# Encoder on one Trainium2 core: LayerNorm shift in one VectorE instruction, one router copy moved to ScalarE, a shorter reciprocal root

## The chip, the core and the metric

The kernel runs on one core of a Trainium2 chip. A core has five engines that work side by side, each with its own queue of instructions in a fixed order: TensorE (PE in the profile, with its weight loads as PEld), VectorE (DVE), ScalarE (ACT), GpSimd (POOL) and SyncE (SP), which here only issues DMAs. TensorE writes to PSUM, and VectorE or ScalarE carry results from PSUM to SBUF. The metric is the device time of one execution in microseconds, taken as the median of several runs.

## The reference, cut to what matters

Two layers over 512 tokens of width 1024. Each layer has a mixer (differential attention in layer 0, sparse latent attention in layer 1), a cross attention to a memory, and a mixture of 16 experts, each followed by a residual and a LayerNorm:

```
def layer_norm(x, g, b):
    mu = mean(x);  xc = x - mu
    return xc * rsqrt(mean(xc * xc) + LN_EPS) * g + b

h = layer_norm(alpha * h + mix, ln_g[i, 0], ln_b[i, 0])
h = layer_norm(alpha * h + memory_cross_attention(h, ...), ln_g[i, 1], ln_b[i, 1])
h = layer_norm(alpha * h + hierarchical_moe(h, ...), ln_g[i, 2], ln_b[i, 2])
```

The root also stands in the RMS norm that follows each head of the differential attention, and in two RMS norms of the latent attention. The mixture's router takes the normalised rows times a 1024x20 matrix, picks a group and two experts for each token, and each expert works on the tokens that chose it.

## The kernel before

Tokens are worked in 4 tiles of 128. Most matmuls are done three times with operands split in a high and a low part ("h" and "l" tiles: ScalarE writes the high part, L203 and L253, VectorE the low one, L204 and L254).

**Order of work.** The instructions of SP and GpSimd run in program order everywhere. Those of TensorE, ScalarE and VectorE are laid out by a planner ahead of the run, with its own estimate of durations, except in three places where the program's order holds: TensorE in the memory attention, all three engines in the expert loop of `moe`, and VectorE in the LayerNorm that ends `moe` (the strings `LNO` give that order: A adds the last expert, C scales, R is a root, H shifts, T turns a tile).

**The root**, `rsqrt` (L183 to L197), is computed on VectorE from an integer seed (L187 to L189) and three Newton steps. A step is L194, L195, L196 where the operand has several columns, and L192, L196 where it has one. So a root is 12 instructions with several columns and 9 with one. Each waits for the one before it. It is used by `attend` of the differential attention (4 columns, tiles rsyrms, one for each of 8 heads; L495 multiplies the head by it and L498 turns the head on TensorE), by `ln_stats` in `out_proj` (1 column, one for each of 16 tiles), by `compress` of the latent attention (2 columns, 4 times) and by the LayerNorm that ends `moe` (layer 0: 1 and 3 columns, layer 1: 2 and 2).

**`out_proj`** (L320 to L347) runs four times: after the mixer (tiles op0x in layer 0, op1x in layer 1) and after the memory attention (xp0x, xp1x). For each half hf of the columns and each tile t it projects (L248 to L250), adds the residual on VectorE (L337), and with hf = 1 takes the statistics (mean L295, squares on ScalarE L299, root), scales in place (L303) and shifts in place. The shift is `ln_shift`: VectorE does 768 of the 1024 columns (L309), GpSimd the last 256 in two instructions (L312, L313). Then:

- after the mixer, `after0` stores the tile to h_d from GpSimd's queue (L1575), and `to_T` turns it on TensorE in eight 128-column transposes (L263) for the memory attention's query projection (xq). The last two transposes read the columns of GpSimd.
- after the memory attention, `after1` stores the tile twice: to h_d from GpSimd's queue (L1584) and to acc_d from SP's (L1585). The expert loop's weight loads (cell_r, L228) stand behind the first acc_d store in SP's queue. Here `router_part` also runs: four transposes of each half (L693), a copy of the result from PSUM (first half on ScalarE L698, second half on VectorE L696), and four matmuls with the router's matrix (L701). `router_logits` (L709 to L711) puts the logits together. The scale L303 overwrites the rows that L693 reads, so it comes after the transposes.

Then VectorE works out the routing (`router`, from L740 on, and the first experts' token lists L889), and GpSimd gathers the first expert's tokens from h_d (L932), which needs all four stores to h_d. The gathered rows are turned on TensorE (L939), split, and the expert loop begins with L954.

In the LayerNorm that ends `moe` the shift already is one VectorE instruction of 1024 columns (`TLNS` = 1024).

Of the kernel before, what the change touches and what calls it, by code (L numbers as in the profile page):

```python
# [17 lines left out]
AF = mybir.ActivationFunctionType  # L18
ALU = mybir.AluOpType
# [4 lines left out]
D = 1024  # L24
# [22 lines left out]
       "A0 A1 C0 A2 R02 C1 A3 H0 H1 C2 R24 C3 H2 H3")  # L47
DSA = ("F2 E2 q0 q1 F3 E3 q2 s0 s1 q3 s2 s3 u0 u1 u2 u3 "
       "k0 k1 k2 k3 k4 k5 k6 k7 v0 v1 v2 v3 x1 a0 x2 a1 x3 a2 a3")
LNS = 768  # L50
TLNS = 1024
SCT = 4
WB = 6
RB = 3
# [11 lines left out]
def encoder(ctx: ExitStack, tc: tile.TileContext, I, out):  # L66
    nc = tc.nc
# [8 lines left out]
    def tp(name):  # L76
        return ps.tile([P, 512], F32, tag="tp", name=name, bufs=2)
# [6 lines left out]
    def t4(tag, name, shape=None, dtype=F32):  # L84
        return sb.tile(shape or [P, 1024], dtype, tag=tag, name=name, bufs=BUFS[tag])

    def t2(tag, name, shape=None, dtype=F32):
        return sb.tile(shape or [P, 512], dtype, tag=tag, name=name, bufs=BUFS[tag])
# [17 lines left out]
    def small(name, shape, dtype=F32, bufs=2):  # L106
        return sb.tile(shape, dtype, tag="_" + re.sub(r"\d+", "", name), name=name, bufs=bufs)
# [74 lines left out]

    def rsqrt(x, n, name, mul, add, room=None):  # L183

        v, y, w, yi = (small(f"rs{q}{name}", [P, room or n], I32 if q == "i" else F32)[:, 0:n] for q in "vywi")
        k = 2.0 ** 26
        nc.vector.tensor_scalar(v, x, mul * k, add * k, op0=ALU.mult, op1=ALU.add)  # L187
        nc.vector.tensor_scalar(yi, v.bitcast(I32), 1, None, op0=ALU.logical_shift_right)  # L188
        nc.vector.tensor_scalar(y.bitcast(I32), yi, -1, 0x5F3759DF - 2 ** 31, op0=ALU.mult, op1=ALU.add)  # L189
        for c in (3.0, 12.0, 768.0):  # L190
            if n == 1:
                nc.vector.scalar_tensor_tensor(w, y, v, y, op0=ALU.mult, op1=ALU.mult)  # L192
            else:
                nc.vector.tensor_tensor(w, y, y, op=ALU.mult)  # L194
                nc.vector.tensor_tensor(w, w, v, op=ALU.mult)  # L195
            nc.vector.scalar_tensor_tensor(y, w, -c, y, op0=ALU.add, op1=ALU.mult)  # L196
        return y  # L197

    def wsplit(raw, hi, lo, scale=None, chunks=1):
# [42 lines left out]
    def ts(t):  # L242
        return slice(t * P, (t + 1) * P)
# [48 lines left out]
    def ln_stats(hx, sums, name, eps=EPS):  # L292
        nmu = small(name + "m", [P, 1])
        if len(sums) == 2:
            nc.vector.tensor_scalar(nmu, sums[0], sums[1], -1.0 / D, op0=ALU.add, op1=ALU.mult)  # L295
        else:
            nc.vector.tensor_scalar(nmu, sums[0], -1.0 / D, None, op0=ALU.mult)
        ss = small(name + "s", [P, 1])
        nc.scalar.activation(junk, hx, AF.Square, bias=nmu, accum_out=ss)  # L299
        return nmu, rsqrt(ss, 1, name, 1.0 / D, eps)  # L300

    def ln_scale(hx, nmu, gb):
        nc.vector.scalar_tensor_tensor(hx, hx, nmu, gb[0], op0=ALU.add, op1=ALU.mult)  # L303

    last_shift = [None]

    def ln_shift(hx, rstd, gb, n=LNS):
        c = slice(0, n)
        last = nc.vector.scalar_tensor_tensor(hx[:, c], hx[:, c], rstd, gb[1][:, c], op0=ALU.mult, op1=ALU.add)  # L309
        if n < D:  # L310
            c = slice(n, D)
            nc.gpsimd.tensor_scalar(hx[:, c], hx[:, c], rstd, None, op0=ALU.mult)  # L312
            nc.gpsimd.tensor_tensor(hx[:, c], hx[:, c], gb[1][:, c], op=ALU.add)  # L313
        last_shift[0] = last

    def proj_part(o, oT, W, t, ks, last=False):
        mm3(o, [(oT[0](k, ts(t)), oT[1](k, ts(t)),
# [33 lines left out]
    def reload(src, name, tags="abcd", q=nc.gpsimd, t0=0):  # L351
        hx = []
        for t, tag in enumerate(tags, t0):
            x = t4(tag, f"{name}{t}")
            q.dma_start(x, src[ts(t), :])  # L355
            hx.append(x)
        return hx


    def diff_attention(x_ap):  # L360
# [92 lines left out]
        def attend(h):  # L453
# [4 lines left out]
            for t in range(NT):  # L458
# [30 lines left out]
                for kt in range(t + 1):  # L489
                    nc.tensor.matmul(po[:, 0:P], pT[:, ts(kt)], V[:, kt, :], start=kt == 0, stop=kt == t)  # L490
                nc.scalar.activation(og[:, t, :], po[:, 0:P], AF.Copy, scale=rs[:, 0:1])
                nc.scalar.activation(junk[:, 0:P], po[:, 0:P], AF.Square, scale=rs[:, 0:1],
                                     accum_out=ssq[:, t:t + 1])
            rstd = rsqrt(ssq, NT, f"rms{h}", 1.0 / P, EPS)
            nc.vector.tensor_tensor(og, og, rstd.unsqueeze(2).to_broadcast([P, NT, P]), op=ALU.mult)  # L495
            pt = tp(f"oT{h}")
# [193 lines left out]
    def router_part(R, t, hf, x, nm):  # L690
        pt = tp(f"hTf{nm}")
        for j in range(4):
            nc.tensor.transpose(pt[:, ts(j)], x[:, ts(j)], ident)  # L693
        xT = t2("e", f"hTs{nm}")
        if hf:
            nc.vector.tensor_copy(xT, pt)  # L696
        else:
            nc.scalar.activation(xT, pt, AF.Copy)  # L698
        lp = tp(f"lg{nm}")
        for j in range(4):  # L700
            nc.tensor.matmul(lp[:, 0:20], xT[:, ts(j)], R["w"][:, 4 * hf + j, 0:20], start=j == 0, stop=j == 3)  # L701
        if hf:
            R["lp"] = lp
        else:
            nc.vector.tensor_copy(R["lg"][:, t, :], lp[:, 0:20])
# [326 lines left out]
    def moe(i, R, early, before, store, after, order, first):  # L1032
        rt = router(i, R)
        xg, xT = {}, {}
# [79 lines left out]
        pg, pu, hid, pt, hs, py, R_ = {}, {}, {}, {}, {}, {}, {}  # L1114
# [4 lines left out]
        def way_in(o, cur, p, j):  # L1119
            W, n = take(p, j)  # L1120
            for v in cur:
                if j % 2 == 0:
                    o[v] = mm(f"p{'gu'[j // 2]}{name(v)}")
                ff_in(o[v], j % 2, xT[v], W)
            return n
# [17 lines left out]
        with tc.manual_schedule(engines={ENG.PE, ENG.Activation, ENG.DVE}):  # L1143
# [7 lines left out]
            for p in range(NE):  # L1151
# [11 lines left out]
                n = way_in(pg, cur, p, 0)  # L1163
                if p:
                    refill(n)
                n = way_in(pg, cur, p, 1)
# [10 lines left out]
                n = way_in(pu, cur, p, 2)  # L1177
                if p:
                    refill(n)
                n = way_in(pu, cur, p, 3)  # L1180
# [38 lines left out]
        hx = reload(acc_d, f"mhx{i}", "aaab")  # L1219
        gb = (t4("c", f"mg{i}"), t4("b", f"mb{i}"))  # L1220
# [22 lines left out]
        rstd = {}  # L1243

        def root(r):
            y = rsqrt(ss[:, r], r.stop - r.start, f"mln{i}{r.start}", 1.0 / D, EPS / ALPHA ** 2, NT)
            for t in range(r.start, r.stop):
                rstd[t] = y[:, t - r.start:t - r.start + 1]

        steps = dict(A=add, C=lambda t: ln_scale(hx[t], nmu[:, t:t + 1], gb),  # L1250
                     H=lambda t: (ln_shift(hx[t], rstd[t], gb, TLNS), store(t, hx[t])))
        before()
        with tc.manual_schedule(engines={ENG.DVE}):
            begin()
# [316 lines left out]
    for i in range(nl):  # L1571
# [29 lines left out]
        def before():  # L1601
            if i + 1 < nl:
                gT.extend([Tall("gTh"), Tall("gTl")])
                D3.extend(dsa(gT, W3))

        def store(t, h):
            if i + 1 == nl:
                nc.sync.dma_start(out[0, ts(t), :], h)
            else:
                nc.sync.dma_start(h2_d[ts(t), :], h)  # L1610

        def after2(st, hx):
# [4 lines left out]
            else:  # L1617
                D3[0](st)

        moe(i, R, early, before, store, after2, LNO[i], first)  # L1620
        if i + 1 < nl:
            D3[0](DSA)
# [28 lines left out]
```

## Time and profile before

| | |
|---|---|
| median of 3 runs | 1695.44 us (1695.03 to 1698.78) |
| the profiled execution | 1692.59 us |
| its span, first to last instruction | 1690.8 us |
| TensorE busy | 1522.3 us (90%) |
| VectorE busy | 1206.2 us (71%), 2381 instructions |
| ScalarE busy | 862.6 us (51%), 1156 instructions |
| GpSimd busy | 230.2 us (14%), 228 instructions |
| mean granted TensorE clock | 0.95 of full |

The spans of the profile count from its first instruction. The profiled execution has 1.8 us around its span, and is 0.17% below the median of the runs. In the rows further down, a time ahead of a row is its start in us from the start of the span; "idle before" is the time in which that engine had nothing to do just ahead, with what ended it.

### The profile page before, as it was taken

How to read it: one execution, taken by the hardware profiler on the slowest of the kernel's cores; microseconds unless marked ns; L12 is line 12 of the kernel's file. 1: busy time of each engine (PE TensorE's matmuls, PEld its weight loads, DVE VectorE, ACT ScalarE, POOL GpSimd, SP SyncE). 2: the span in 40 equal slices, each digit the busy share in tenths (PEclk: the TensorE clock that was granted, in tenths of full speed). 3: DMA queues.
4: the chain of work that ended last, by engine and by line, in shares of the span. 5: the costliest groups of instructions: out<-in, count | busy, mean ns of one | idle time of the engine just before them, and what ended most of it. 6: DMA issues, size and time to landing. Idle time of an engine off the chain costs nothing. (4 is left out here: it accounts for less than half of the span.)

```text
span 1690.8 us, 23295 instructions
## 1 busy us (share of the span) xinstructions
PE 1522.3 (90%) x8572; PEld 1292.7 (76%) x8572; DVE 1206.2 (71%) x2381; ACT 862.6 (51%) x1156; POOL 230.2 (14%) x228
## 2 busy tenths in 40 slices
PE   7998799698995899999996899998998699999994
PEld 7988699597784777888875757698777487888883
DVE  5555746555447998898875698836436899899795
ACT  5443646432320775775763454533322477677671
POOL 1000000011004031231210000002002222132120
PEclk9999899799996899999997999999998699999998
DMA  7210234432415798998974301024242599899883
GB/s 227 75 51 1 75 113 157 156 91 87 165 59 213 246 364 314 311 355 314 320 254 157 96 25 63 26 89 151 76 142 110 211 363 371 281 333 368 280 300 124
DMA packets 118334, 317.58 MB, mean 188 GB/s; under 512 B 23773, under 2 KB 72925, under 8 KB 93632
## 3 DMA queue, kind: packets, MB, share of 16 engines
q1 hardware_dynamic: 100400, 272.00, 45.3%
q0 software_dynamic: 17808, 43.96, 8.5%
q8 instruction: 71, 1.16, 0.3%
q14 instruction: 55, 0.45, 0.1%
HBM read 299.38 MB, written 36.70 MB: 199 GB/s over the span
## 5 line engine op out<-in xcount | busy, mean ns | idle before, releaser
L204 DVE TENSOR_TENSOR cell_l<-cell_r,cell_h 128x2048 fp32r<-128x2048 f32 x192 | 430.7, 2285 | 40.4 <-ACT cell_h L203 39.9
L203 ACT ACTIVATE cell_h<-cell_r 128x2048 fp32r<-128x2048 f32 x192 | 363.4, 1915 | 77.7 <-DMA cell_r<-in_moe_w_up_dram 17.8
L954 PE MATMUL pg<-cell_h,xh 128*128 128x512 f32 x288 | 118.9, 413 | 2.2 <-ACT xh L253 2.2
L982 PE MATMUL py<-cell_h,hsh 128*128 128x512 f32 x288 | 115.4, 401 | 1.4 <-ACT hsh L253 0.7
L954 PE MATMUL pg<-cell_l,xh 128*128 128x512 f32 x288 | 116.2, 403 | 0.0
L982 PE MATMUL py<-cell_h,hsl 128*128 128x512 f32 x288 | 112.8, 392 | 0.0
L982 PE MATMUL py<-cell_l,hsh 128*128 128x512 f32 x288 | 112.5, 390 | 0.0
L954 PE MATMUL pu<-cell_h,xh 128*128 128x512 f32 x288 | 112.0, 389 | 0.0
L954 PE MATMUL pu<-cell_l,xh 128*128 128x512 f32 x288 | 112.0, 389 | 0.0
L972 POOL DMA_INDIRECT acc_d<-y,sx x34 | 72.9, 2143 | 152.1 <-ACT y L971 103.2
L932 POOL DMA_INDIRECT xg<-h_d,sx x32 | 42.0, 1312 | 363.8 <-DVE sx L919 334.2
L253 ACT ACTIVATE xh<-xgT 128x1024 fp32r<-128x1024 f32 x36 | 36.9, 1024 | 101.6 <-PE xgT L939 95.9
L954 PE MATMUL pg<-cell_h,xl 128*128 128x512 f32 x288 | 79.8, 400 | 0.0
L954 PE MATMUL pu<-cell_h,xl 128*128 128x512 f32 x288 | 77.0, 389 | 0.0
L954 PEld LDWEIGHTS pg<-cell_h,xh 128*128 128x128 f32 x288 | 56.6, 197 | 14.1 <-ACT xh L253 3.0
L954 PEld LDWEIGHTS pg<-cell_h,xl 128*128 128x128 f32 x288 | 56.1, 195 | 12.5
L954 PEld LDWEIGHTS pg<-cell_l,xh 128*128 128x128 f32 x288 | 56.3, 195 | 11.4
L982 PEld LDWEIGHTS py<-cell_h,hsh 128*128 128x128 f32 x288 | 54.2, 188 | 13.0 <-DVE xl L254 1.0
L982 PEld LDWEIGHTS py<-cell_h,hsl 128*128 128x128 f32 x288 | 54.0, 188 | 12.5 <-DVE hsl L254 0.4
L954 PEld LDWEIGHTS pu<-cell_h,xh 128*128 128x128 f32 x288 | 54.1, 188 | 11.2
L954 PEld LDWEIGHTS pu<-cell_h,xl 128*128 128x128 f32 x288 | 54.1, 188 | 11.2
L954 PEld LDWEIGHTS pu<-cell_l,xh 128*128 128x128 f32 x288 | 54.1, 188 | 11.2
(918 smaller groups left out, 4203.9 us busy)
## 6 DMA issues: line engine op xcount, KB each, us to landing
cell_r<-in_moe_w_gate_dram SPq DMA_DIRECT2D x64, 1024.0 KB, 7.8
cell_r<-in_moe_w_up_dram SPq DMA_DIRECT2D x64, 1024.0 KB, 7.8
cell_r<-in_moe_w_down_dram SPq DMA_DIRECT2D x64, 1024.0 KB, 6.9
mhx<-acc_d POOLq DMA_DIRECT2D x8, 512.0 KB, 7.4
x<-in_x_dram SPq DMA_DIRECT2D x4, 512.0 KB, 6.7
g<-in_ln_g_dram POOLq DMA_DIRECT2D x4, 512.0 KB, 4.0
b<-in_ln_b_dram POOLq DMA_DIRECT2D x4, 512.0 KB, 3.9
op0x<-in_x_dram POOLq DMA_DIRECT2D x4, 512.0 KB, 5.2
```

The lines of the kernel that those rows point to most:

```text
L203: nc.scalar.activation(hi[:, c], raw[:, c], AF.Copy)
L204: nc.vector.tensor_tensor(lo[:, c], raw[:, c], hi[:, c].bitcast(F32), op=ALU.subtract)
L253: nc.scalar.activation(hi, src, AF.Copy)
L932: nc.gpsimd.indirect_dma_start(out=x, out_offset=None, in_=h_d[:, :], in_offset=bass.IndirectOffsetOnAxis(ap=idx[:, 0:1], axis=0), bounds_ ...
L954: nc.tensor.matmul(o, xT[l][:, a, :], W[r][:, k, :], start=a == l == r == 0, stop=a == 7 and l == 1)
L972: nc.gpsimd.indirect_dma_start(out=acc_d[:, :], out_offset=bass.IndirectOffsetOnAxis(ap=ix[:, 0:1], axis=0), in_=y, in_offset=None, bounds ...
L982: nc.tensor.matmul(o, hs[a][:, ts(2 * q + f)], Dq[b][:, f, c], start=q == f == k == 0, stop=q == f == 1 and k == 2)
```

## The change

Three edits. The shift of a LayerNorm is one VectorE instruction over all 1024 columns in every place; the two GpSimd instructions go. The router's second half is copied from PSUM by ScalarE, as the first half is. The root has one third-order step and one Newton step in place of three Newton steps: 8 instructions with one column, 10 with several.

```diff
     def rsqrt(x, n, name, mul, add, room=None):
         v, y, w, yi = (...)
-        k = 2.0 ** 26
+        k = (1024.0 / 27.0) ** 2
         nc.vector.tensor_scalar(v, x, mul * k, add * k, op0=ALU.mult, op1=ALU.add)
         nc.vector.tensor_scalar(yi, v.bitcast(I32), 1, None, op0=ALU.logical_shift_right)
         nc.vector.tensor_scalar(y.bitcast(I32), yi, -1, 0x5F3759DF - 2 ** 31, op0=ALU.mult, op1=ALU.add)
-        for c in (3.0, 12.0, 768.0):
+        for cubic in (True, False):
             if n == 1:
                 nc.vector.scalar_tensor_tensor(w, y, v, y, op0=ALU.mult, op1=ALU.mult)
             else:
                 nc.vector.tensor_tensor(w, y, y, op=ALU.mult)
                 nc.vector.tensor_tensor(w, w, v, op=ALU.mult)
-            nc.vector.scalar_tensor_tensor(y, w, -c, y, op0=ALU.add, op1=ALU.mult)
+            if cubic:
+                nc.vector.scalar_tensor_tensor(w, w, -10.0 / 3.0, w, op0=ALU.add, op1=ALU.mult)
+            nc.vector.scalar_tensor_tensor(y, w, 5.0 if cubic else -64.0 / 3.0, y, op0=ALU.add, op1=ALU.mult)
         return y
...
-    def ln_shift(hx, rstd, gb, n=LNS):
-        c = slice(0, n)
-        last = nc.vector.scalar_tensor_tensor(hx[:, c], hx[:, c], rstd, gb[1][:, c], op0=ALU.mult, op1=ALU.add)
-        if n < D:
-            c = slice(n, D)
-            nc.gpsimd.tensor_scalar(hx[:, c], hx[:, c], rstd, None, op0=ALU.mult)
-            nc.gpsimd.tensor_tensor(hx[:, c], hx[:, c], gb[1][:, c], op=ALU.add)
-        last_shift[0] = last
+    def ln_shift(hx, rstd, gb):
+        last_shift[0] = nc.vector.scalar_tensor_tensor(hx, hx, rstd, gb[1], op0=ALU.mult, op1=ALU.add)
...
         xT = t2("e", f"hTs{nm}")
-        if hf:
-            nc.vector.tensor_copy(xT, pt)
-        else:
-            nc.scalar.activation(xT, pt, AF.Copy)
+        nc.scalar.activation(xT, pt, AF.Copy)
...
-                     H=lambda t: (ln_shift(hx[t], rstd[t], gb, TLNS), store(t, hx[t])))
+                     H=lambda t: (ln_shift(hx[t], rstd[t], gb), store(t, hx[t])))
```

## Rows read from the trace of the kernel before

**Rows 1.** Busy time by stretch: us, PE, PEld, DVE, ACT, POOL, clock, DMA share, GB/s.

```profile
550.00:895.00 345.00, 333.85 (x1589) 272.87 (x1590) 303.00 (x400) 237.12 (x179) 71.78 (x54) 0.99 0.88 312
```

**Rows 2.** PE waits, 0 to 355 us: waited for, us in total, times, longest.

```profile
PE oT L498 <- DVE og L495: 17.7, 4, 4.6
```

**Rows 3.** Timeline of TensorE at the ends of the LayerNorms: start, us, engine, instruction.

```profile
371.63 0.44 PE L263 MATMUL hT<-ident,op0x 128*128 128x128 f32 x2 [1.25 <-POOL op0x L313]
...
391.36 0.88 PE L263 MATMUL hT<-ident,op0x 128*128 128x128 f32 x6 [0.98 <-DVE op0x L309]
392.95 0.44 PE L263 MATMUL hT<-ident,op0x 128*128 128x128 f32 x2 [0.72 <-POOL op0x L313]
...
908.56 1.97 PE L263 MATMUL gT<-ident,mhx 128*128 128x128 f32 x8 [12.69 <-DVE mhx L309]
...
1173.33 0.44 PE L263 MATMUL hT<-ident,op1x 128*128 128x128 f32 x2 [0.42 <-POOL op1x L313]
```

**Rows 4.** Timeline of VectorE, after the memory attention of layer 0.

```profile
514.59 0.69 DVE L696 COPY hTsxp<-hTfxp 128x512 f32<-128x512 f32 x1 [0.30 <-PE hTfxp L693]
515.20 1.28 DVE L303 SCALAR_TENSOR_TENSOR xp0x<-xp0x,xp0ln0m,g 128x1024 f32<-128x1024 f32 x1
...
531.59 0.16 DVE L740 TENSOR_REDUCE rt<-lgs 128x4 f32<-128x16 f32 x1
...
539.37 0.16 DVE L889 TENSOR_SCALAR ix<-pi 128x1 int32<-128x1 f32 x1 [0.28 <-PE pi L887]
```

**Rows 5.** Timeline of GpSimd, same stage.

```profile
533.56 0.61 POOL L1584 DMA_DIRECT2D h_d<-xp0x  x1 [0.30 <-POOL xp0x L313]
...
542.48 1.08 POOL L932 DMA_INDIRECT xg<-h_d,ix  x1 [6.46 <-DVE rt L792]
```

**Rows 6.** Line 932, 500 to 560 us: the gather's wait in its queue, ns.

```profile
L932 POOLq EVENT_SEMAPHORE  x3: 17/43/7857, 533.7 to 542.3; - x3
```

**Rows 7.** The chain that ended last, near its end: start, us, what.

```profile
1682.64 0.17 DVE rswmln L194
```

**Rows 8.** Timeline of VectorE, one root with 4 columns (attention) and one with 1.

```profile
329.34 0.16 DVE L196 SCALAR_TENSOR_TENSOR rsyrms<-rswrms,rsyrms 128x4 f32<-128x4 f32 x1
329.53 0.69 DVE L495 TENSOR_TENSOR og<-og,rsyrms 128x512 f32<-128x512 f32 x1
...
389.83 0.22 DVE L192 SCALAR_TENSOR_TENSOR rswop0ln<-rsyop0ln,rsvop0ln 128x1 f32<-128x1 f32 x1
390.09 0.16 DVE L196 SCALAR_TENSOR_TENSOR rsyop0ln<-rswop0ln,rsyop0ln 128x1 f32<-128x1 f32 x1
```

**Rows 9.** Line 309 of VectorE: ns min/median/max, first and last start, shapes.

```profile
L309 DVE SCALAR_TENSOR_TENSOR mhx<-mhx,rsymln,mb x8: 1274/1280/1285, 907.2 to 1685.5; 128x1024 f32<-128x1024 f32 x8
L309 DVE SCALAR_TENSOR_TENSOR op0x<-op0x,rsyop0ln,b x4: 1008/1019/1066, 368.2 to 390.3; 128x768 f32<-128x768 f32 x4
```

**Rows 10.** Timeline, a GpSimd addition and the VectorE instruction beside it, layer 0's mixer.

```profile
386.62 0.87 POOL L313 TENSOR_TENSOR op0x<-op0x,b 128x256 f32<-128x256 f32 x1
...
386.82 1.75 DVE L303 SCALAR_TENSOR_TENSOR op0x<-op0x,op0ln3m,g 128x1024 f32<-128x1024 f32 x1
```

**Rows 11.** Busy time by stretch (columns as in Rows 1), xq matmuls of layers 0 and 1.

```profile
396.00:399.00 3.00, 3.00 (x18) 3.00 (x17) 0.10 (x1) 0.00 (x0) 0.00 (x0) 0.59 0.00 0
...
1176.00:1180.00 4.00, 4.00 (x36) 4.00 (x35) 0.48 (x1) 0.60 (x1) 0.00 (x0) 1.00 0.01 2
```

**Rows 12.** Line 698 of ScalarE: ns min/median/max, first and last start, shapes.

```profile
L698 ACT ACTIVATE hTsxp<-hTfxp x8: 597/598/598, 489.4 to 1287.2; 128x512 f32<-128x512 f32 x8
```

**Rows 13.** SyncE's queue, the store that stands ahead of the weight loads.

```profile
519.15 0.33 SPq L1585 DMA_DIRECT2D acc_d<-xp0x  x1
```

**Rows 14.** Busy time by stretch (columns as in Rows 1), where the transfers end.

```profile
541.00:542.00 1.00, 0.00 (x0) 0.00 (x0) 0.90 (x6) 0.00 (x0) 0.00 (x0) 0.50 0.34 135
```

**Rows 15.** DMA queues, 517 to 545 us: packets, MB, share of 16 engines.

```profile
q1 hardware_dynamic: 1152, 6.29, 58.1%
q0 software_dynamic: 666, 2.17, 20.3%
```

More of the change, by code (lines that the diff above doesn't have):

```diff
@@ L49 @@
        "k0 k1 k2 k3 k4 k5 k6 k7 v0 v1 v2 v3 x1 a0 x2 a1 x3 a2 a3")
-LNS = 768
-TLNS = 1024
 SCT = 4
```

## The prediction

> **What bounds the kernel now.** I read the busy time by stretch first, then the waits of TensorE, then the timelines of the places that those waits name, and the chain that ended last for the end. In the expert loops, about 345 us in layer 0 and nearly as long in layer 1, TensorE is busy 334 of 345 us [rows 1]: no edit touches them, and what begins earlier ahead of them ends earlier by as much. The changed instructions matter only in the joints between, and there are three kinds.
>
> In the attention of layer 0 TensorE stands still 17.7 us in four waits for the head that VectorE multiplies by its root [rows 2]. Four heads of eight wait; the other four are covered by other matmuls.
>
> At the ends of the LayerNorms TensorE waits for rows to turn [rows 3]. After layer 0's mixer the first tile's last two transposes wait 1.25 us for GpSimd, and the last tile waits 0.98 us for VectorE's shift and then 0.72 us for GpSimd's. In layer 1 one wait of 0.42 us for GpSimd is left. At the start of layer 1 the wait of 12.69 us ends with a shift, ahead of which stands a root.
>
> After the memory attention VectorE works nearly without a pause from 514.59 to 531.59 us, where the routing begins, and the first token list is ready some 8 us later [rows 4]. GpSimd issues its last store to h_d at 533.56 and gathers at 542.48 [rows 5]; the gather had waited 7.86 us in the queue, until 542.3 [rows 6]. The list was there by 539.6, so it is the store's landing that ends this wait last. Layer 1 repeats the pattern. At the very end the root's instructions stand one by one on the chain [rows 7]; the order string puts two roots there.
>
> **The root.** With several columns an instruction takes a step of 0.19 us (from 329.34 to 329.53) [rows 8], and two fall away: 0.38 us. With one column, the dropped step is one L192 (0.26 us from 389.83 to 390.09) and one L196, and the third-order step adds one of L196's kind: 0.26 us saved. Where it lies on the path: four heads, 4 x 0.38 = 1.5 us; two roots of the end, 0.8 us; the one-column root ahead of the 12.69 us wait, 0.3 us. The four roots of the latent attention's norms are worth 0 to 1.5 us; no wait that I show ends with them, so I take 0.4 us. The other roots lie beside other work and count nothing; the worst they could cost is nothing, since each is shorter.
>
> **The shift after the mixers.** VectorE's instruction grows from 1.019 to 1.280 us [rows 9]: +0.26 us for each tile, which the shorter root gives back. GpSimd's two instructions vanish, and with them the wait of the last two transposes. Besides, an L303 that ran beside a GpSimd addition took 1.75 us in place of 1.28 [rows 4, 10], so 0.47 us of stall goes too. Layer 0, first tile: 1.25 us, and +0.26 - 0.26 = 0. Last tile: 0.72 us, and of the 0.98 us before it 0.26 + 0.47 - 0.26 = 0.47; together 1.2 us. After that tile the granted clock was 0.59 on the mean, so mostly at the lower level of 1.2 GHz (18 matmuls in 3 us); in layer 1, where the pauses ahead of it were shorter by about those amounts, it stayed at 1.00, 2.4 GHz (36 in 4 us) [rows 11]. 18 x (0.167 - 0.111) = 1.0 us; I take it, since the pauses that are left come near to layer 1's. Layer 0: 3.45 us, between 1.25 (the last tile waits on something else) and 4. Layer 1: 0.42 us, taken as 0.4. The h_d store behind it now waits for VectorE alone; it is read long after and hidden.
>
> **The stage after the memory attention**, twice. From VectorE's 17.0 us [rows 4] go four copies at a step of 0.61 us (514.59 to 515.20), 2.4 us; stalls beside four GpSimd additions, from 0 to 4 x 0.47, taken as three, 1.4 us; two roots, half hidden in each other, 0.3 us. Four longer shifts add 1.0 us. Net 3.1 us: the routing begins near 528.5 and the first list is ready near 536.4. The copy itself takes 0.60 us on ScalarE [rows 12] against 0.69 on VectorE, so the matmuls behind it lose nothing; behind it in ScalarE's queue stands at most the next tile's squares, which the root of that tile waits for. Should a copy stand behind such a square it is late once, by about its 0.6 us or two of them, which the next tile's transposes would feel: 0 to 1.2 us, taken as 0, because the scale L303 waits for the transposes and not for the copy.
>
> The last store to h_d goes out right after the last shift, near 528.8 in place of 533.56: 4.8 us earlier. If it lands as long after its issue as before (542.3 - 533.56 = 8.7 us), the gather starts 4.8 us earlier: the upper end. But the transfers are what is full here. They start with the first store to acc_d, at 519.15 [rows 13], behind which the weight loads stand in SP's queue, and end a third of the way into 541 to 542 [rows 14]. That first store follows the first tile's shift, and in the new order it goes out near 517.2: L303 begins 0.6 us earlier without the copy, and the store no longer waits for GpSimd's second instruction. If the same bytes need the same 22.2 us, they end 2.0 us earlier: the lower end. The lists, 3 us earlier, are ready before that. I take 2.9 us, nearer to the lower end because the bytes have to pass in any case: 5.8 us for both layers.
>
> How the two queues share is open. In this stage GpSimd's queue q0 moved 666 packets of 2.17 MB and SP's q1 1152 of 6.29 MB [rows 15], and the last store took 8.7 us though at most one other stood ahead of it in q0. The Trainium skill, "DMA: Bandwidth & Descriptors", section "Queues, rings and completion order", says that a DMA engine goes round the queues that have work, one packet of one queue at a time. By that rule the h_d stores would overtake the weight loads and the sum would be the first rival's, 1676.5 us; by the 8.7 us of the row, which bear it out in part only, it is the one here.
>
> **The sum.** 1.5 + 0.8 + 0.3 + 0.4 + 3.45 + 0.4 + 5.8 = 12.65 us. The profiled execution's 1692.6 us become 1679.9; it lies 0.17% below the median of the runs, so on the median 1695.4 - 12.7 = 1682.7, given as 1683. Changes of under 0.2% (3.4 us) are about what a measurement of this kernel can't tell from none.
>
> **Rivals.** *The stores overtake the loads.* The packets are 3.3 KB on q0 and 5.5 KB on q1 [rows 15]. If the queues take turns packet by packet, q0 has 3.3 of 8.8, 37% of 381 GB/s (8.46 MB in 22.2 us), and its last two stores of 0.52 MB each are through in 7.4 us, near 534 if the first of them goes out near 526. Then the list, near 536.4, starts the gather, 6.1 us earlier than 542.48, and two stages give 12.2 in place of 5.8: 1676.5 us. For it: more of q0's stores are queued early. Against it: the 8.7 us of the last store. Chance 0.13.
>
> *The transfers end where they did.* If something other than the first shift holds back the loads, or the loads, now ahead, delay the stores, the two stages give nothing: 1683 + 5.8 = 1688.5 us. For it: transfers were still running in 541 to 542 [rows 14] with the gather behind them. Chance 0.15.
>
> *The planner lays the engines out anew.* Outside the hand-ordered parts it works from its own durations, and shorter roots and other engines give it other input. Place: the heads of layer 0's attention. Price: a head whose turn is put right behind its root costs 17.7 / 4 = 4.4 us [rows 2]; four heads have none of this now. With two or three of them uncovered, 8.8 to 13.3 us are lost, and the time is 1691.5 to 1696: no change within 0.2% (chance 0.12, with smaller disorders elsewhere). With all four, 17.7 us, it is 1700 us and slower; that is the point from which it decides (chance 0.08). For it: the planner did uncover four heads already. Against it: the edit removes two of the twelve small instructions and moves nothing that a head waits for.
>
> The forecast itself has 0.52, with a range of its own from 1677 to 1689: the lower and upper ends above (layer 0's joint 1.25 to 4, each routing stage 2.0 to 4.8, the latent norms 0 to 1.5). Faster: 0.52 + 0.13 + 0.15 = 0.80; same 0.12; slower 0.08. The range, 1674 to 1693, takes in both faster rivals and the lower edge of no change, and leaves out some 0.18.
>
> **What would show it.** Right: 2326 instructions on VectorE (2381 - 17 - 30 - 8), 1164 on ScalarE and 196 on GpSimd; no wait of TensorE for GpSimd in front of L263; the four waits behind L495 each 0.4 us shorter; no L303 over 1.3 us; the clock at 1.00 after layer 0's last tile; routing begun 3 us sooner after the first tile's transposes and the gather 2 to 5 us sooner; two roots 0.8 us shorter at the end; the expert loops as long as before. Wrong: more or longer waits behind L495, a gather that still waits as long after the first shift, a router matmul that waits on ScalarE, or an expert loop of another length.

## The result and the profile after

| | kernel before | changed kernel |
|---|---|---|
| median of the runs | 1696.80 us (5 runs, 1695.03 to 1698.78) | 1686.36 us (5 runs, 1682.32 to 1688.29) |
| ratio | 1 | 0.9933, 95% interval 0.9919 to 0.9947 |
| profiled execution | 1692.59 us, span 1690.8 | 1682.87 us, span 1680.7 |
| instructions on VectorE / ScalarE / GpSimd | 2381 / 1156 / 228 | 2325 / 1165 / 196 |

By the ratio the kernel is 11.4 us faster (0.67%, 9.0 to 13.7); the two medians differ by 10.4. The forecast was 12.65 us, 1683 us on the median before. The profile after, read at the places that the forecast named. First TensorE's waits behind the root of the attention, one row for each head that waits (in brackets the wait and what ended it):

```profile
130.70 0.71 PE L493 MATMUL oT<-ident,og 128*128 128x128 f32 x4 [4.20 <-DVE og L490]
...
182.46 1.08 PE L493 MATMUL oT<-ident,og 128*128 128x128 f32 x4 [4.18 <-DVE og L490]
...
308.99 1.09 PE L493 MATMUL oT<-ident,og 128*128 128x128 f32 x4 [10.30 <-DVE og L490]
...
326.50 1.09 PE L493 MATMUL oT<-ident,og 128*128 128x128 f32 x4 [3.61 <-DVE og L490]
```

Three of the four that [rows 2] sums are 0.39 to 0.40 us shorter (in the kernel before they were 4.60, 4.57 and 4.00). The third grew from 4.49 to 10.30; a wait of 2.95 us for an exponential, which stood just ahead of it in the kernel before, is in that:

```profile
304.98 2.07 PE L466 MATMUL sc<-kS,qab 128*128 128x512 f32 x4 [2.95 <-ACT p L475]
...
311.54 1.12 PE L498 MATMUL oT<-ident,og 128*128 128x128 f32 x4 [4.49 <-DVE og L495]
```

So the four together grew, from 17.7 us to 22.3.

Second, the joint after layer 0's mixer. TensorE's timeline has two long waits in it (and two of 0.69 and 0.34 us at the last tile), and none is for GpSimd:

```profile
375.33 0.38 PE L249 MATMUL xq<-hTh,xwq00h 128*128 128x256 f32 x1 [2.17 <-ACT hTh L254]
...
378.94 0.58 PE L250 MATMUL xq<-hTl,xwq00h 128*128 128x256 f32 x1 [3.22 <-DVE hTl L255]
```

The waits of [rows 3] behind the shift are gone, but the first query product now waits for the high and the low part of tile 1. ScalarE's and VectorE's timelines say why:

```profile
371.11 1.90 ACT L204 ACTIVATE xwq01h<-xwq01r 128x2048 fp32r<-128x2048 f32 x1
372.91 1.89 ACT L204 ACTIVATE xwq02h<-xwq02r 128x2048 fp32r<-128x2048 f32 x1
374.71 0.58 ACT L254 ACTIVATE hTh<-hT 128x512 fp32r<-128x512 f32 x1
...
375.92 2.29 DVE L205 TENSOR_TENSOR xwq02l<-xwq02r,xwq02h 128x2048 fp32r<-128x2048 f32 x1
...
378.20 0.69 DVE L255 TENSOR_TENSOR hTl<-hT,hTh 128x512 fp32r<-128x512 f32 x1
```

Both engines split the weights of two later query products first. In the kernel before, one part of tile 1 stood between the two splits, and TensorE's two waits for tile 1, both for low parts, were 1.6 and 2.0 us:

```profile
376.42 1.90 ACT L203 ACTIVATE xwq01h<-xwq01r 128x2048 fp32r<-128x2048 f32 x1
378.22 0.57 ACT L253 ACTIVATE hTh<-hT 128x512 fp32r<-128x512 f32 x1
379.56 1.91 ACT L203 ACTIVATE xwq02h<-xwq02r 128x2048 fp32r<-128x2048 f32 x1 [0.77 <-PE op0o L249]
...
381.40 0.39 PE L249 MATMUL xq<-hTl,xwq00h 128*128 128x256 f32 x1 [1.63 <-DVE hTl L254]
...
385.05 0.39 PE L249 MATMUL xq<-hTl,xwq00h 128*128 128x256 f32 x1 [1.96 <-DVE hTl L254]
```

The clock behind the last tile, 0.59 in [rows 11], is at full speed here, but the stretch at the lower level is not gone: it now stands behind the wait of 3.22 us (windows of layer 0; columns: stretch, busy us of PE, PEld, DVE, ACT and POOL, granted clock, DMA share, GB/s):

```profile
379.00:383.00 4.00, 4.00 (x19) 4.00 (x20) 3.86 (x10) 1.64 (x3) 0.53 (x1) 0.50 1.05 391
...
386.00:392.00 6.00, 4.97 (x40) 4.54 (x39) 2.56 (x4) 1.19 (x2) 0.53 (x1) 1.00 0.21 87
392.00:396.00 4.00, 4.00 (x35) 4.00 (x35) 0.00 (x0) 0.61 (x2) 0.00 (x0) 1.00 0.02 4
```

Over the whole joint the granted clock was 0.91 in the changed kernel and 0.96 in the kernel before:

```profile
354.90:393.23 38.33, 31.91 (x244) 31.05 (x243) 26.72 (x62) 13.02 (x19) 2.14 (x4) 0.91 0.50 167
```

```profile
359.06:399.40 40.34, 32.11 (x245) 30.42 (x244) 27.44 (x66) 13.13 (x18) 12.47 (x12) 0.96 0.48 159
```

Third, the stage after layer 0's memory attention, on SP, GpSimd and VectorE:

```profile
511.18 0.33 SPq L1577 DMA_DIRECT2D acc_d<-xp0x  x1
...
523.61 0.16 DVE L732 TENSOR_REDUCE rt<-lgs 128x4 f32<-128x16 f32 x1
...
523.99 0.53 POOL L1576 DMA_DIRECT2D h_d<-xp0x  x1 [1.45 <-DVE rt L734]
524.51 1.86 POOL L920 MEMSET xg<- 128x1024 f32 x2
...
524.72 1.68 DVE L736 TENSOR_SCALAR rt<-rt 128x16 f32<-128x16 f32 x1
...
532.27 0.16 DVE L881 TENSOR_SCALAR ix<-pi 128x1 int32<-128x1 f32 x1 [0.28 <-PE pi L879]
...
534.00 1.08 POOL L924 DMA_INDIRECT xg<-h_d,ix  x1 [7.64 <-DVE rt L771]
```

Beside [rows 4, 5, 13] the first store to acc_d goes out 7.97 us sooner, the last one to h_d 9.57, the list is ready 7.10 and the gather starts 8.48 us sooner; 6.17 us of each come from further ahead (the first copy of a query product is at 393.23 us in place of 399.40).

### The profile page after: what moved, and what is told of

Read it like the earlier page. It is cut to its first block, busy times and chain, and to the rows that moved or that the text cites. A ratio compares the mean times of both kernels' runs of the same rounds, so it can differ in the third digit from the quotient of the medians.

```text
span 1680.7 us, 23201 instructions
## 1 busy us (share of the span) xinstructions
PE 1518.5 (90%) x8572; PEld 1290.8 (77%) x8572; DVE 1195.1 (71%) x2325; ACT 866.8 (52%) x1165; POOL 192.2 (11%) x196
## 5 line engine op out<-in xcount | busy, mean ns | idle before, releaser
L254 ACT ACTIVATE xh<-xgT 128x1024 fp32r<-128x1024 f32 x36 | 36.8, 1022 | 91.8 <-PE xgT L931 91.8
```

The lines of the kernel that those rows point to most:

```text
L254: nc.scalar.activation(hi, src, AF.Copy)
```

## The experiments

One profile of each kernel is not enough to split 11 us into parts, so the stages are given for all profiles that share a stage's program. Stage lengths in us, from the timelines: "attention" ends with the first mean of op0x, a "joint" goes from the first mean of op0x or op1x to the first copy of a query product, "to gather" from there to the first gather, "end" from the first product that adds the last expert (L1236 in the kernel before) to the start of the last two shifts.

```
                         attention   joint 0   to gather   joint 1   to gather   end
before                     359.06     40.34     143.08      36.78     143.00    19.92
before again               359.62     39.95     143.35      39.97     142.83    19.95
root alone                 359.62     39.97     143.20      36.86     143.21    19.17
root alone again           358.50     40.22     143.20      40.44     143.20    19.15
root alone, third          359.34     40.07     143.21      37.17     143.24    19.27
shift alone                359.90     38.21     141.80      41.31     142.02    19.90
copy alone                 359.89     39.70     142.63      40.13     142.72    19.94
changed kernel             354.90     38.33     140.77      38.79     139.56    19.09
changed, loads later       355.48     38.43     143.59      38.58     141.53    19.10
changed, acc_d twice       358.76     39.06     140.35      38.74     140.22    19.08
changed, gate              359.87     35.72     140.64      36.23     139.85    19.11
before, turn deferred      348.60     39.53     143.57      37.21     143.14    20.30
gate, turn deferred        346.73     36.63     140.90      33.38     139.68    19.08
the same, router first     349.28     33.39     140.88      33.40     139.89    19.70
```

**The three parts alone.** The kernel before with one part of the change each (only the first lines of each part are shown, the rest is as in the change).

```diff
 # root alone
-        for c in (3.0, 12.0, 768.0):
+        for cubic in (True, False):
...
 # shift alone
-    def ln_shift(hx, rstd, gb, n=LNS):
+    def ln_shift(hx, rstd, gb):
...
 # copy alone
-        if hf:
-            nc.vector.tensor_copy(xT, pt)
-        else:
-            nc.scalar.activation(xT, pt, AF.Copy)
+        nc.scalar.activation(xT, pt, AF.Copy)
```

> The kernel before with the new root alone (one third-order and one Newton step), shift and router copy as before. Theory A, the sum of the prediction: four heads of the attention give 1.5 us, the two roots of the end 0.8, the rest at most 1; the run is 3 us shorter than before (ratio 0.998), and the start of layer 0's output projection moves by 1.5 us. Theory B, the planner lays the attention out anew as soon as the root is shorter: all of the 4.16 us by which the changed kernel's attention ended sooner is there with this edit alone, TensorE's waits behind the multiplication by the root differ in number and place and not by 0.4 us each, and the run is 5 to 6 us shorter (ratio 0.997). The waits of 1.25, 0.98 and 0.72 us for GpSimd and VectorE at layer 0's last transposes stay in both.

> The kernel before with the shift wholly on VectorE alone. Theory A, the sum: nothing changes up to layer 0's output projection; there the waits for GpSimd go, 1.25 us at the first tile and 0.72 + 0.47 at the last, less 0.26 for each longer shift, and with the clock 1.0 us: 2.5 to 3.5 us, in layer 1 0 to 0.4; in the stage after each memory attention the last store to h_d goes out some 2 to 4 us sooner and the gather 1 to 2 us sooner. Sum 5 to 8 us (ratio 0.996). Theory B: the 2.0 us that the changed kernel lost in layer 1's joint belong to the longer shift, so layer 1's joint is 1.5 to 2 us longer here too and layer 0's gains only 2; sum 3 to 4 us. Theory C: the loss there needs the shorter root as well, and layer 1's joint keeps its length here.

> The kernel before with the router's turned halves all copied by ScalarE, root and shift as before. Nothing changes ahead of layer 0's memory attention. VectorE has four copies of 0.61 us less in the stage behind it. If the transfers decide, the gather follows the first store to acc_d, which goes out 0.6 us sooner: 0.6 us for each layer, 1.2 us in all (ratio 0.9993). If the list and the last store's issue decide, 2.4 us for each layer, 4.8 in all (ratio 0.997). GpSimd's parts of the shift still stretch VectorE's scales to 1.75 us.

Measured, as ratio to the kernel before: root 0.9952 (0.9934 to 0.9970), 8.1 us; shift 0.9976 (0.9967 to 0.9986), 4.1 us; copy 0.9994 (0.9985 to 1.0003), 1 us, which is not told from none. Shift and copy come out near their lower theories in size: the shift gives joint 0 1.8 us and the ways to the gather 0.9 to 1.4, the copy gives these 0.2 to 0.6. With the shift alone joint 1 took 41.31 us, 1.3 more than in a profile of the kernel before with the same waits for loads (below); its clock was lower there, 0.52 where that profile has 1.00:

```profile
1160.00:1170.00 10.00, 8.18 (x36) 7.89 (x37) 9.11 (x24) 2.15 (x4) 0.54 (x1) 0.52 0.87 310
```

Whether the longer shift brings that about or the execution, one profile can't tell. The root's 8 us are more than either theory. Its profiles were all of executions of 1693.1 to 1695.6 us, while its runs go down to 1683.5, and they show some 0.5 us in the attention, 0.7 at the end and 1.6 in the latent attention between the first turned row and the output projection (198.1 to 198.2 us in three profiles, 199.6 and 200.0 before). The rest goes with the clock: the two shortest of the eight runs, 1683.5 and 1684.3 us, had a mean granted clock of 0.952 and 0.953, the two longest, 1692.0 and 1693.1 us, had 0.944, and the four between lie between. What gives some executions the higher clock stays open, since none of them was profiled.

**The root alone, profiled again and a third time** (the same program).

> The same program as the kernel with the new root alone, profiled a second time, because its first profile was of its slowest execution (1693.1 us of 1683.5 to 1693.1) and shows none of the 8 us that the runs show. Theory A, the root's gain lies in TensorE's clock: in a faster execution the same instructions stand in the same order, the attention ends several us sooner than in the first profile, and the granted clock in 100 to 200 us and 300 to 340 us is higher there. Theory B, the gain lies behind the attention: the output projection starts at the same time as in the first profile (359.6 us for the first mean) and the difference builds up later.

> The kernel with the new root alone, profiled a third time; the two profiles so far were of slow executions (1693.1 and 1695.6 us, where the runs go from 1683.5). If a fast execution is caught (under 1689 us): theory A, the attention ends 2 to 5 us sooner than in the two profiles at a higher granted clock (first mean at 354 to 356 us); theory B, the joint of layer 1 takes 36.9 us and the expert loops are 2 to 3 us shorter. If it is slow again, the stages repeat those of the first two within 1 us but for the joint of layer 1, which takes 36.9 or 40.4.

Measured: 1695.6 and 1693.4 us, so no short execution was caught. But up to the first mean the root alone, the changed kernel and its first three variants in the table have TensorE's matmuls in the same order, and the seven profiles of that order end the attention anywhere from 354.90 to 359.87 us. Two of them, the changed kernel and the gated one, in the windows of 170 to 200 us:

```profile
170.00:200.00 30.00, 20.30 (x117) 16.40 (x117) 21.94 (x58) 21.39 (x60) 0.00 (x0) 0.89 0.15 47
```

```profile
170.00:200.00 30.00, 21.00 (x102) 17.44 (x102) 20.54 (x62) 20.00 (x55) 0.00 (x0) 0.72 0.11 36
```

The first had the clock at 0.89, the second at 0.72, with the same order of matmuls. Summed up to the output projection's first product, TensorE is busy 269.5 us in the one and 274.8 in the other, and idle 42.9 and 41.8. So the 5 us between them are mostly time at the lower clock, not waits, and so are most of the 4.16 us of "gain" in the changed kernel's one profile. The mean of the seven, 358.1, against 359.6 for the four of the old order, is 1.5 us.

**The kernel before, profiled a second time.**

> The kernel before, profiled a second time, to see how far its stages move from one execution to the next. Theory A (the joint of layer 1 grew by 2 us with the change): from the first mean to the first query copy it takes 36 to 37.5 us again, against 38.6 to 38.8 in three profiles of the changed order. Theory B (the first profile was one in which TensorE's clock fell less): it takes 38 to 41 us here, and the granted clock behind the last tile is lower than in the first profile. Attention: 358.5 to 360 us at the first mean in both.

Measured: joint 1 took 39.97 us, so the 2 us that I had read as a loss in layer 1 are not the change's. The cause is not the clock, either. VectorE's timeline of this second profile, at the first tile of op1x:

```profile
1144.61 0.33 DVE L679 TENSOR_TENSOR wg<-wr,gc 128x160 f32<-128x160 f32 x1 [2.58 <-DMA gc<-in_ln_g_dram]
1146.89 0.33 DVE L679 TENSOR_TENSOR wg<-wr,gc 128x160 f32<-128x160 f32 x1 [1.95 <-DMA gc<-in_ln_b_dram]
1147.13 0.15 DVE L187 TENSOR_SCALAR rsvop1ln<-op1ln0s 128x1 f32<-128x1 f32 x1
```

and of the first:

```profile
1144.44 0.70 DVE L679 TENSOR_TENSOR wg<-wr,gc 128x160 f32<-128x160 f32 x2 [2.71 <-DMA gc<-in_ln_g_dram]
1145.05 0.15 DVE L187 TENSOR_SCALAR rsvop1ln<-op1ln0s 128x1 f32<-128x1 f32 x1
```

The two products of the router's weights with small loaded vectors stand in VectorE's queue ahead of the first tile's root. In one execution the second vector was there in time, in the other it came 1.95 us later, and TensorE then also waited 1.25 us for GpSimd at the first tile, as in layer 0. It goes through the table: where joint 1 took 36.8 to 37.2 us this second wait was 0 to 0.6 us, where it took 40 us and more, 1.4 to 2.1. The changed kernel had it in its three profiles (1.4 to 2.0 us). Compared at like waits, 39.97 and 40.13 us (the copy alone) with GpSimd's part of the shift, 38.58 to 38.79 after, joint 1 gained 1.3 us.

**The gate.** The splits of the second and third query weight are queued behind the last tile's turned halves, on ScalarE and VectorE (`gate` holds the two instructions of the last `split_evac`).

```diff
             to_T(h, hT, t, f"hT{i}{t}")
+            turned[i] = list(gate)
...
+            if h in (1, 2):
+                with tc.issue_after(turned[i][0].ins), tc.issue_after(turned[i][1].ins):
+                    W = U.get(f"xwq{nm}")
...
```

> The changed kernel with the splits of the second and third query weight of each memory attention (two of 1.9 us on ScalarE, two of 2.29 us on VectorE) queued behind the last tile's turned halves; nothing else is changed. Theory A, the weight splits are what cost the joints after the mixers: TensorE's waits of 2.17 and 3.22 us in layer 0 and 2.33 and 3.22 us in layer 1 ahead of the first query product shrink to under 1 us each, each joint is 3 to 5 us shorter than in the changed kernel, and the run is near 1678 us on the median (ratio to before 0.988 to 0.990). Theory B, the last tile's norm ends the joint in any case, or the second query product now waits for its weights: the joints are 0 to 1 us shorter, or longer, and the run stays within 2 us of the changed kernel's 1686 us (ratio 0.993).

Measured: 0.9918 (0.9902 to 0.9934), 1682.9 us; joints 35.72 and 36.23 us, 2.6 and, at a like wait for the router's load (1.9 us), 2.4 to 2.6 us shorter than in the changed kernel. TensorE's waits of the joint of layer 0, first in the changed kernel:

```profile
PE xq L250 <- DVE hTl L255: 3.6, 2, 3.2
PE xq L249 <- ACT hTh L254: 2.9, 2, 2.2
```

and with the gate:

```profile
PE hT L265 <- DVE op0x L311: 1.8, 1, 1.8
PE xq L249 <- ACT hTh L254: 1.4, 2, 0.7
PE xs L597 <- DVE xQ L582: 1.2, 1, 1.2
PE xq L250 <- DVE hTl L254: 0.3, 1, 0.3
```

The waits for tile 1 shrank as theory A says. A wait of 1.8 us for the third tile's shift took part of their place, and one of 1.2 us, 0.4 in the changed kernel, stands just behind the joint; so the joints gain less than the 3 to 5 us of theory A, and the run stays 5 us above its 1678. The joints' gain is shown; against the changed kernel the medians differ by 3.5 us, the ratios by 2.5, within the scatter of the attention.

**What ends the wait ahead of the gather.** Two variants of the changed kernel: the experts' first loads behind the third and fourth tile, and every tile stored once more to a buffer that is not read; one execution of each, 1687.8 and 1693.9 us.

```diff
 # loads later
-            if t < NFIRST:
+            t -= NT - NFIRST
+            if t >= 0:
 # acc_d twice
             nc.sync.dma_start(acc_d[ts(t), :], h)
+            nc.sync.dma_start(acc2_d[ts(t), :], h)
...
```

> The changed kernel with the experts' first weight loads and splits issued behind the third and fourth tile of the stage after the memory attention, not behind the first and second. In the changed kernel the gather followed the first store to acc_d by 22.8 us (layer 0) and 21.6 us (layer 1) and began 1.7 and 1.2 us after its list. Theory A, the transfers still end the wait: the stores to h_d no longer share with the loads, and the gather starts 0.5 us sooner in layer 0, right behind its list. Theory B, in the changed kernel the list has taken over as the last to come: the gather does not move against its list by more than 0.3 us. In both, the weights come later, and if that is later than the first expert wants them, TensorE waits for a DMA there, up to 5 us.

> The changed kernel with every tile of the stage after the memory attention stored to acc_d and once more to a buffer that nothing reads: 2.1 MB more on the same queue, 4.9 us at the 430 GB/s that the stage moves. Theory A, the transfers end the wait ahead of the gather: the gather follows the first store by 1.2 us more (one doubled store stands ahead of the last loads) up to 4.9 us more, in place of 22.8 and 21.6 us, while the list stays. Theory B, the list ends it: the distance stays within 0.3 us.

Measured, by the DMA issues (KB of each, us from issue to landing). Loads later, a store to h_d issued while no load runs, with only a store to acc_d beside it, and the last one, right behind the loads:

```profile
h_d<-xp0x POOLq DMA_DIRECT2D x1, 512.0 KB, 3.8
...
h_d<-xp0x POOLq DMA_DIRECT2D x1, 512.0 KB, 11.8
```

Acc_d twice, the last one:

```profile
h_d<-xp0x POOLq DMA_DIRECT2D x1, 512.0 KB, 8.4
```

In the changed kernel the last one took 9.1 us, in the kernel before 8.0:

```profile
h_d<-xp0x POOLq DMA_DIRECT2D x1, 512.0 KB, 9.1
```

```profile
h_d<-xp0x POOLq DMA_DIRECT2D x1, 512.0 KB, 8.0
```

With the loads later, the gather started 4.5 us behind its list, at 537.50, which is 0.95 us behind the landing (524.75 + 11.8): the store decides, and beside the loads it takes three times as long as beside a store to acc_d. With 2.1 MB more on SP's queue the last store took no longer, and the gather stood 22.4 us behind the first store to acc_d, not 24 to 28 (in layer 1 22.3 in place of 21.6, its last store having gone out 0.9 us later behind the first): the sum of the bytes does not decide. They cost something behind the gather, where the first expert's products came after 10.5 and 8.9 us in place of 7.4 and 6.3. In this variant the list (537.1) and the landing (528.83 + 8.4 = 537.2) come together, so it does not tell the two apart. But in both layers of the kernel before, the changed kernel and the two variants the gather starts 0.8 to 0.95 us behind the landing of the last store, while it starts 1.0 to 4.5 us behind its list. So both single theories fall, and the landing ends the wait; in the changed kernel, with the landing at 533.1 and the list at 532.4, it is nearly a tie.

**The turn of a head behind its filling work.** The four transposes of a head are emitted after the projections that fill the gap, on the gated kernel and on the kernel before (at head 6 the splits of the heads turned so far move behind the turn too).

```diff
-            attend(h)
+            og = attend(h)
             for f in FILL[h]:
                 ...
+            turn(h, og)
...
```

> The gated kernel with the turn of each head of layer 0's attention (the four transposes behind the root) emitted after the head's filling projections, so that the planner has other matmuls to put between the root and the turn. Theory A, TensorE's waits behind the root (22.3 us in four in the changed kernel) are on the path: they shrink to under 8 us, the attention ends 8 to 14 us sooner, and the run is near 1672 us (ratio to before 0.986 or less). Theory B, what is pulled ahead of the turn is missing later: the waits move to the exponentials and to the transposes of the weights, and the run stays within 3 us of the gated kernel's 1683 us.

> The kernel before (old root, old shift, old router copy, no gate) with the turn of each head emitted after the head's filling projections, as in the kernel where that stood on top of the change and the gate and gave 15 us. Theory A, the deferred turn and the change are independent but for the two heads whose wait it removes: the run is 11 to 15 us shorter than before (ratio 0.991 to 0.993), with the first mean of layer 0 at 346 to 350 us in place of 359 to 360. Theory B, the shorter root is what lets the planner place the turns well: with the old root the waits behind the root stay near 17.7 us, and the gain is under 5 us.

Measured: 0.9815 (0.9792 to 0.9839), 1667.1 us with change and gate; 0.9931 (0.9910 to 0.9951), 1684.6 us on the kernel before. The gains are those of theory A, but not by its route. TensorE's waits behind the root, over 90 to 340 us, with change and gate:

```profile
PE oT L498 <- DVE og L492: 16.8, 3, 9.5
```

They did not shrink to under 8 us, and on the kernel before they are 18.3 us in four beside 17.7 in [rows 2]. What shrank is elsewhere: TensorE is idle 35.8 and 35.7 us up to the output projection's first product, in place of 42.0 in the kernel before (47.6 of 50 us busy in 100 to 150 us, in place of 40.9), and busy 4.4 us less, the clock having been at 0.97 there in place of 0.93. From 1684.6 to 1667.1 us are 17.5 (19.7 by the ratios), so change and gate lose nothing of their 13.9 us to it.

**The router's loads first**, on top of all this.

```diff
+        wr = router_load(i)
         out_proj(oT, h2_d if i else x_ap, (i, 0), f"op{i}", after0)
-        wr = router_load(i)
```

> The kernel with change, gate and deferred turns, and with the router's small loads (weights, biases, norm scales) issued ahead of the output projection's loads, not behind the second weight load of the memory attention. In the profiles VectorE stands in front of the router's weight product 2.4 to 3.0 us for the first of these loads in layer 1 (3.6 to 4.7 in layer 0) and in some executions 1.4 to 2.0 us more for the second, with the first tile's root queued behind it. Theory A, that wait is what moved layer 1's joint between 36.8 and 40.0 us with one and the same program: it is gone, layer 1's joint takes 30 to 32 us in place of 33.4 to 36.2, layer 0's 33 to 35 in place of 36.6, and the run is 3 to 6 us shorter than the 1667 us of the kernel it stands on. Theory B, the first tile's squares end the wait in any case (1.36 us at the second tile): under 1 us a layer, 1665 to 1667 us.

Measured: 0.9822 (0.9807 to 0.9837), 1667.1 us, nothing gained. Joint 0 fell by 3.2 us to 33.39, as theory A says, joint 1 stayed at 33.4 (the second wait was absent in the profile without this edit too), but the attention grew by 2.6:

```profile
318.48 0.33 DVE L684 TENSOR_TENSOR wg<-wr,gc 128x160 f32<-128x160 f32 x1 [2.93 <-DMA gc<-in_ln_g_dram]
...
320.01 0.69 DVE L492 TENSOR_TENSOR og<-og,rsyrms 128x512 f32<-128x512 f32 x1
```

The planner moved the router's product ahead of the last head's root, and VectorE waits for the same load there: TensorE's wait behind that root is 6.86 us in place of 3.61.

## Why the forecast was right, step by step

The total was right (12.65 forecast, 11.4 measured), in part by luck. Of its terms the end's was right in place and size, layer 0's joint failed by 2 us, layer 1's came out 0.9 us above, the stages' was right in size by another weighing than the one named, and the attention's is not shown. Taken edit by edit the agreement is poor: the root's terms add up to 3 us, and the root alone measured 8.1, of which its profiles show about 3 and the rest goes with the clock.

- **Attention, 1.5 us.** Three waits are 0.4 us shorter, as the step says. The fourth was laid out anew, in the place that the third rival named, at 10.30 - 4.49 - 2.95 = 2.9 us for one head in place of 4.4, so the four waits together gave nothing. TensorE's idle time up to the output projection was 42.9 us beside 42.0 in the first profiles of the two kernels, and 42.2 beside 43.2 on the mean of the seven profiles of the new order and the four of the old. Over all profiles the stage gained 1.5 us, but with a scatter of 5 us in the new order the agreement can't be called shown.
- **End, 0.8 us.** 19.92 and 19.95 us against 19.08 to 19.11 in the changed kernel and its first three variants: 0.84.
- **Latent norms, 0.4 us, and the root ahead of the 12.69 us wait, 0.3 us.** Neither is visible: between the gather and the turned rows profiles of one kind differ by 2 us, and the 1.6 us that the latent attention gained with the root alone are not there in the changed kernel and its variants (199.5 to 200.6 us).
- **Layer 0's joint, 3.45 us: the term that failed.** It gave 1.4 us (40.0 to 38.6 on the mean). GpSimd's waits went and the clock stayed at 1.00 behind the last tile, as the step says. But the 1.0 us that it put down for the clock was not gained: the stretch at the lower level moved to the matmuls behind tile 1's waits (0.50 over 379 to 383 us), and over the whole joint the clock was 0.91, where the two profiles of the kernel before have 0.96 and 0.91. And it missed what is late next: the planner put both weight splits ahead of tile 1's halves. The gate takes that out and brings some 2.5 us back in each layer, so the cause is shown. The bound of 1.25 us that the step gave was the right end to take.
- **Layer 1's joint, 0.4 us.** 1.3 us at like waits. The row on which the step rested, one wait of 0.42 us, was of an execution in which a small load came early; in the other profile of the kernel before TensorE waited 1.25 and 0.35 us at the first tile.
- **The stages after the memory attention, 5.8 us.** 2.3 and 3.4 us at the gather, 5.8 with both up to the first expert's products (2.45 and 3.34). The size is right and the weighing is not. I had 2.0 us as the lower end because the same bytes need the same time behind the first store; acc_d twice refutes that. The landing of the last store to h_d decides, as in the upper end. That store went out 3.4 us sooner in the stage of layer 0 and 4.3 in that of layer 1, where the step has 4.8, and it took 1.1 and 0.9 us longer to land (9.1 us in place of 8.0, 8.7 in place of 7.8); what is left are the 2.3 and 3.4 us. The step's 8.7 us for the landing count to the end of the gather's wait, 0.7 us behind the landing itself. That the mean of the two stages is just the 2.9 us taken between the ends is luck. The list itself came only 0.9 us sooner in the stage, not 3.0: the routing began 1.8 us sooner, and a stall of 1.5 us (L736 above, 1.68 in place of 0.17 us), with one of 0.6 us in the kernel before (L735, 0.73 us), took half of that back.
- **The first rival, 6.1 us a stage.** Not so. The Trainium skill, "DMA: Bandwidth & Descriptors", section "Queues, rings and completion order", says that the engines go round the queues packet by packet. That queueing more on SP's queue did not delay GpSimd's stores (8.4 us beside 9.1) agrees with it; the share that follows from the packet sizes does not: the last two stores of the changed kernel went out at 522.00 and 523.99 us and were through at 533.1, 11.1 us after the first of them, where 7.4 was worked out. The second rival, in which the stages give nothing, falls with the 2.3 and 3.4 us.

## What to carry to other kernels

Profile a kernel more than once before reading a gain of a few us from one stage: here one order of matmuls ended the attention 5 us apart, mostly by the clock, and one program ended a joint 3 us apart by a 2 us wait for a small load. When an edit takes a wait away in a stage that a planner lays out, look in the new order for large work without a due time (weight splits) that now stands ahead of small work that is due, and queue it behind. Instructions that only prepare a later step and wait for a small load should not stand in front of the root on an in-order engine; and where only the load was moved here, the planner moved its consumer too, and the wait with it.

## What was not expected of the hardware

- A 16-column VectorE instruction took 1.68 us beside two GpSimd memsets and ended with the second (524.72 + 1.68 = 526.40, 524.51 + 1.86 = 526.37); another, on two operands, begun at 524.51, took its usual 0.17. The Trainium skill, "SBUF — State Buffer", section "SBUF: two separate sides", says that VectorE and GpSimd share a port pair which one of them holds for a whole instruction while the other is blocked, and that a VectorE instruction with two inputs is concerned only against a GpSimd instruction that reads SBUF. These rows agree with it, the memset having no input; that the wait lasted through both memsets is more than it says. In the kernel before, the memsets began at 534.16, behind the same instruction (533.33, 0.17 us), and held nothing up.
- A store of 512 KB to h_d landed after 3.8 us where only a store to acc_d ran beside it, and the last store ahead of the gather after 7.8 to 11.8 us beside the weight loads; 2.1 MB more on SP's queue did not lengthen that (8.4 us).
- The granted clock of one and the same order of matmuls was 0.89 or 0.72 over 170 to 200 us, in different executions; busy time followed it, idle time did not.
